# A hybrid attention layer on one core: weight splits behind the first norm, zeroing behind the norms, one early load for the expanding matrix

## The chip, the cores and the metric

The kernel runs on one core of a Trainium2 chip. TensorE (PE) multiplies, VectorE (DVE), ScalarE (ACT) and GpSimd (POOL) compute on vectors, SyncE (SP) issues the DMAs. Each engine takes its instructions in order and waits on semaphores for the others. The metric is the time of one execution on the device in microseconds; lower is better.

## What is computed

One layer: an RMS norm of x, one wide projection, three attention mixers (A, B, C) with gates, and an output projection. S = 512, D = 1024, heads of 64, everything in float32.

```python
hn = rms_norm(x, ln_g[l])
proj = jnp.einsum('bsd,dc->bsc', hn, w_in[l])
...
qa = rms_norm(qa.reshape(b, s, H_A, HEAD_DIM), g[0])
ka = rms_norm(ka.reshape(b, s, H_A, HEAD_DIM), g[1])
o_a = moba_attention(qa, ka, va.reshape(b, s, H_A, HEAD_DIM), rel_bias[OFF_A:OFF_A + H_A])
...
branches = jnp.stack([o_a.reshape(b, s, W_BR) * jax.nn.silu(ga),
                      o_b.reshape(b, s, W_BR) * jax.nn.silu(gb),
                      o_c.reshape(b, s, W_BR) * jax.nn.silu(gc)], axis=2)
br = jnp.einsum('bsiw,iwd->bsid', branches, w_branch[l])
gates = jax.nn.sigmoid(gate_logits.reshape(b, s, N_BRANCH, D_MODEL))
merged = jnp.sum(gates * br, axis=2)
x = x + jnp.einsum('bsd,de->bse', merged, w_out[l])
```

## The kernel before

Every matrix product is made of three: each float32 operand is split into a high part (hi, rounded to PE's float32r) and a low part (lo, the rest), and PE adds hi*hi, hi*lo and lo*hi. The hi part is a cast, mostly on ACT (`split_hi`, L135), the lo part a subtraction on DVE or POOL (`split_lo`, L140).

The opening (`start_x`) loads x in four tiles of 128 rows. For each, ACT squares and sums it (L211), DVE adds the epsilon (rvx, L144), POOL takes the power -0.5 (rrx, L146), DVE scales by that and by the norm's weights (xn, two halves, L216; lng are the weights spread over the partitions by PE), PE transposes xn into pt and xsc (L222), and ACT and DVE split the result into xhi and xlo. The first unit's weights (`load_w`, two k steps of 128 by 512 columns in a tile w of 128x1024, four tiles, then two tiles for V) are split too. With `early` set, DVE makes hi of every second tile (L137) and POOL lo of the others.

The work then goes through units A0, W0, R0, Z0 and so on. `project` makes q and k of a unit, four tiles t of 24 matmuls each (L500 to L502), and V in four more of half the width. After each tile of q and k, ACT copies and squares it (qn, sq), DVE sums by head (ss, L516) and adds the epsilon (rv), POOL takes the power (rr), DVE scales (qn, L527), and PE transposes (tr, L557). V's result is split straight from PSUM, in four pieces, in turn on ACT and DVE. PSUM holds two such results (pj). A0's projection is run alone; W0's fills PE during A0's attention.

`start_bias`, traced behind A0's projection, builds the rows of the position bias: a one-hot table (o32, cast to oh by POOL), a mask (mk), a small matmul (pf), and an addition (fb) that goes to DRAM scratch, from which attention loads bt. It also loads and casts emat, the matrix with which `spread` later expands a value per head to 64 columns. ws and wst are buffers of `spread` whose unused parts are zeroed once, from zer.

The order on each engine is set by a scheduler when the kernel is built; `tc.issue_after(ins)` makes the instructions in its block follow ins on ins's engine, without a semaphore. Buffers with one tag are reused in turn (`oraw` has three), so a load into one waits for the last use of what was there.

Of the kernel before, what the change touches and what calls it, by code (L numbers as in the profile page):

```python
# [9 lines left out]
F32 = mybir.dt.float32  # L10
F32R = mybir.dt.float32r
AF = mybir.ActivationFunctionType
ALU = mybir.AluOpType
# [4 lines left out]
S = 512  # L18
D = 1024
NT = 4  # L20
KT = 8
BIG = 1e30
EPS = 1e-6
WBUFS = 6
LBUFS = 4
ORAWS = 3
# [77 lines left out]
def body(tc, x, ln_g, w_in, qk_g, sinks, w_branch, w_out, rel_bias, c_ident, c_onehot, c_mask, c_expand, out):  # L104
    nc = tc.nc
    V, A, G, T = nc.vector, nc.scalar, nc.gpsimd, nc.tensor
# [7 lines left out]
    with top:  # L114
# [8 lines left out]
        emat = cp.tile([128, 2, 512], F32R, name="emat")  # L123
        mhalf = cp.tile([128, 8], F32, name="mhalf")
# [8 lines left out]
        def split_hi(dst, src, eng=A):  # L133
            if eng is A:
                A.copy(dst, src)  # L135
            else:
                eng.tensor_copy(dst, src)  # L137

        def split_lo(dst, src, hi, eng=V):
            eng.tensor_tensor(dst, src, hi.bitcast(F32), ALU.subtract)  # L140

        def rsqrt(pool, src, n, inv, tag):
            v = pool.tile([128, n], F32, name="rv" + tag, tag="rv" + tag)
            V.tensor_scalar(v, src, inv, EPS, ALU.mult, ALU.add)  # L144
            r = pool.tile([128, n], F32, name="rr" + tag, tag="rr" + tag)
            G.tensor_tensor(r, v, mhalf[:, :n], ALU.pow)  # L146
            return r

        nw = [0]
# [22 lines left out]
        def win_piece(c, n):  # L172
            return (n, lambda k0, k1: win[:, k0:k1, c : c + n])
# [3 lines left out]
        qkv = top.enter_context(tc.tile_pool(name="qkv", bufs=2))  # L177
# [5 lines left out]
        def start_x():  # L183

            lrow = qkv.tile([1, D], F32, name="lrow", tag="vhi")
            nc.sync.dma_start(lrow, ln_g)
            ones = qkv.tile([1, 128], F32, name="ones", tag="sq", bufs=1)
            V.memset(ones, 1.0)
            lng = [ps.tile([128, 512], F32, name="lng", tag="po") for _ in range(2)]
            for g in range(2):  # L190
                T.matmul(lng[g], ones, lrow[:, g * 512 : g * 512 + 512], start=True, stop=True)
            xts = []
            xsc = ps.tile([128, 2, 512], F32, name="xsc", tag="sc", bufs=1)

            def load_x(t):
                xt = qkv.tile([128, D], F32, name="xt", tag=("qhi", "qlo")[t % 2])
                nc.sync.dma_start(xt, x2[t * 128 : (t + 1) * 128, :])
                xts.append(xt)

            load_x(0)  # L200
            nc.sync.dma_start(idr, c_ident)
            for t in range(NT):
                if t == 1:
                    load_x(1)
                    w = loads(units[0], True)
                    load_x(2)
                    load_x(3)
                xt = xts[t]
                sq = qkv.tile([128, D], F32, name="xsq", tag="klo")
                ss = qkv.tile([128, 1], F32, name="xss", tag="xss")  # L210
                A.activation(sq, xt, AF.Square, accum_out=ss)  # L211
                r = rsqrt(qkv, ss, 1, 1.0 / D, "x")
                xn = qkv.tile([128, D], F32, name="xn", tag="khi")
                for g in range(2):
                    gs = slice(g * 512, g * 512 + 512)
                    V.scalar_tensor_tensor(xn[:, gs], xt[:, gs], r, lng[g], ALU.mult, ALU.mult)  # L216
                    if g:
                        pt = xsc[:, t % 2].rearrange("p (k c) -> p k c", k=4)
                    else:
                        pt = ps.tile([128, 4, 128], F32, name="pt", tag="tr")  # L220
                    for k in range(4):
                        T.transpose(pt[:, k], xn[:, (g * 4 + k) * 128 : (g * 4 + k + 1) * 128], ident)  # L222
                    dh = xhi[:, g * 4 : g * 4 + 4, t * 128 : (t + 1) * 128]
                    dl = xlo[:, g * 4 : g * 4 + 4, t * 128 : (t + 1) * 128]
                    split_hi(dh, pt)
                    split_lo(dl, pt, dh)
            return w

        def start_bias():

            rb = qkv.tile([64, 32], F32, name="rb", tag="qn", bufs=3)
            V.memset(rb, 0.0)
            nc.sync.dma_start(rb[:40, :], rel_bias)
            rp = ps.tile([32, 64], F32, name="rp", tag="po")
            T.transpose(rp, rb, ident[:64, :64])
            rt = qkv.tile([64, 64], F32R, name="rt", tag="qn", bufs=3)
            V.tensor_copy(rt[0:32], rp)
            split_lo(rt[32:64], rp, rt[0:32])
            for kinds in (("A", "W"), ("C", "R", "Z")):
                c0 = OFF[kinds[0]]  # L240
                n = sum(SPAN[k][0] for k in kinds)
                o32 = qkv.tile([64, 1024], F32, name="o32", tag="oraw", bufs=ORAWS)
                oh = qkv.tile([64, 1024], F32R, name="oh", tag="oraw", bufs=ORAWS)
                mk = qkv.tile([8, 1024], F32, name="mk", tag="oraw", bufs=ORAWS)
                fb = qkv.tile([8, 1024], F32, name="fb", tag="oraw", bufs=ORAWS)
                nc.sync.dma_start(o32[:, :n], c_onehot[:, c0 : c0 + n])
                G.tensor_copy(oh[:, :n], o32[:, :n])
                nc.sync.dma_start(mk[:, :n], c_mask[:, c0 : c0 + n])
                for k in kinds:
                    for c in range(0, SPAN[k][0], 512):  # L250
                        m = min(512, SPAN[k][0] - c)
                        o = OFF[k] + c - c0
                        pf = ps.tile([8, 512], F32, name="pf", tag="po")
                        T.matmul(pf[:, :m], rt[:, HEAD0[k] : HEAD0[k] + 8], oh[:, o : o + m], start=True, stop=True)
                        V.tensor_tensor(fb[:, o : o + m], pf[:, :m], mk[:, o : o + m], ALU.add)
                nc.sync.dma_start(scr[:, c0 : c0 + n], fb[:, :n])
            for g in range(2):
                e32 = qkv.tile([128, 512], F32, name="e32", tag="qn", bufs=3)
                nc.sync.dma_start(e32, c_expand[:, g * 512 : g * 512 + 512])
                V.tensor_copy(emat[:, g], e32)  # L260

        def start_small():
            for h in range(2):
# [176 lines left out]
        with att:  # L440
            at = att.enter_context(tc.tile_pool(name="att", bufs=2))

            zer = qkv.tile([128, 128], F32, name="zer", tag="qn", bufs=3)
            V.memset(zer, 0.0)
            revr = at.tile([128, 128], F32R, name="revr", bufs=1)
            identr = at.tile([128, 128], F32R, name="identr", bufs=1)
            ws = at.tile([128, NT, 192], F32R, name="ws", bufs=1)
            for c in range(0, 192, 32):
                G.tensor_copy(ws[:, :, c : c + 32], zer.rearrange("p (t c) -> p t c", t=NT))
            wsts = [at.tile([128, S], F32R, name=f"wst{i}", bufs=1) for i in range(2)]  # L450
            for wt in wsts:
                for c in range(0, S, 128):
                    G.tensor_copy(wt[64:128, c : c + 128], zer[64:128, :])
            pthi = at.tile([128, 1664], F32R, name="pthi", bufs=1)
            ptlo = at.tile([128, 1664], F32R, name="ptlo", bufs=1)
            V.tensor_copy(pthi[:, 1408:1536], zer)
# [396 lines left out]
            units = [(k, int(h), max("WRZ".find(k), 0)) for k, h in UNITS]  # L853

            def loads(unit, early=False):
                kind, hf, gi = unit
                c = hf * 256
                if kind == "C":
                    if hf == 0:
                        return [load_w([win_piece(QC, 256), win_piece(KC, 256)], KT)]  # L860
                    return [load_w([win_piece(QC + 256, 256)], KT)]
                if kind == "A":
                    q, k, v = QA, KA, VA
                else:
                    q, k, v = QB + gi * 512, KB + gi * 512, VB + gi * 512
                qk, vv = [win_piece(q + c, 256), win_piece(k + c, 256)], [win_piece(v + c, 256)]
                if kind in "RZ":
                    return [load_w(vv, KT), load_w(qk, KT)]
                return [load_w(qk, KT, early), load_w(vv, KT)]
# [47 lines left out]
            for ui, (kind, hf, gi) in enumerate(units):  # L917
# [5 lines left out]
                if ui not in uq:  # L923
                    run(unit_project(ui, wnext))
                    if ui == 0:
                        start_bias()
                    wnext = loads(units[ui + 1]) if ui + 1 < len(units) else None
                u = uq[ui]
                oraw = oraw_tile()
# [11 lines left out]
                name = kind + str(hf)  # L941
# [130 lines left out]
        for n in range(2, len(jobs) - 1):  # L1072
# [3 lines left out]
            w, wnext = wnext, job_load(n + 1)  # L1076
# [15 lines left out]
            else:  # L1092
                br = "ABC"[i]
                for dc in range(4):
                    tg = ("pj", "sc", "tr", "po")[dc]
                    po = gsc[0][:, 1] if tg == "sc" else ps.tile([128, 512], F32, name="po", tag=tg)
                    for k in range(4):
                        a = w[0](k)[:, dc * 128 : dc * 128 + 128]
# [77 lines left out]
```

## Time and profile before

| | |
|---|---|
| median of 3 runs (lowest to highest) | 797.91 us (796.34 to 802.05) |
| the profiled execution, its own time | 801.72 us |
| its span | 799.9 us |
| busy PE, DVE, ACT, POOL in the span | 96%, 62%, 52%, 28% |
| mean granted clock of PE | 0.991 of 2.4 GHz |

Rows of the profile name engine, line, operation, what is written and read, and the duration. What stands in square brackets is how long the engine had been idle before it and who released it. Times count from the span's start.

### The profile page before, as it was taken

The numbers are of one execution on the slowest core, as the hardware profiler recorded it, in microseconds if no ns is written. First come the engines' busy times: TensorE is split into PE (matmuls) and PEld (weight loads), VectorE is DVE, ScalarE is ACT, GpSimd is POOL, SyncE is SP. The second block draws the span as 40 slices with busy tenths as digits, with TensorE's granted clock in tenths as the row PEclk, the third lists the DMA queues.
The fourth block names the chain that finished last, engine by engine and source line by source line (L and its number), as shares of the span: only waits on it lengthen the run. The fifth ranks groups of instructions, "written<-read, shape, count | busy, mean of one in ns | idle before, by whom it ended". The sixth has DMA issues, their size and how long they took to land.

```text
span 799.9 us, 12675 instructions
## 1 busy us (share of the span) xinstructions
PE 768.9 (96%) x4727; PEld 658.4 (82%) x4727; DVE 496.9 (62%) x1068; ACT 413.3 (52%) x914; POOL 223.4 (28%) x139
## 2 busy tenths in 40 slices
PE   5989999999999989999999999899999999999998
PEld 3877788788878878878887877688899999999886
DVE  5663554546547665353655785748999787987512
ACT  4542664666566356466656656465455345445300
POOL 5573623261762372326173240101000000000000
PEclk9999999999999999999999999999999999999999
DMA  9343325153322143515332121515044324436302
GB/s 272 119 144 84 105 82 157 60 187 91 106 79 60 54 132 82 157 60 185 93 105 72 54 61 43 168 35 158 27 159 134 102 83 132 132 105 201 116 1 105
DMA packets 67473, 85.99 MB, mean 107 GB/s; under 512 B 4915, under 2 KB 53171, under 8 KB 67412
## 3 DMA queue, kind: packets, MB, share of 16 engines
q1 hardware_dynamic: 67412, 85.19, 35.0%
q8 instruction: 37, 0.61, 0.3%
q14 instruction: 24, 0.20, 0.1%
HBM read 75.67 MB, written 9.50 MB: 106 GB/s over the span
## 4 chain that ended last, share of the span: by engine, by line
PE 89%; DVE 3%; ACT 2%; DMA 2%; POOL 1%; issue 1%; SPq 0%; ACTq 0%; DVEq 0%; POOLq 0%
PE pj L500 12%; PE pj L501 12%; PE pj L502 12%; PE fc L356 11%; PE acc L1130 6%; PE fsc L356 4%; PE po L610 3%; PE pj L276 3%; PE pj L277 3%; PE pj L278 3%; PE sc L660 2%; DMA w<-in_w_in 2%; PE po L1100 2%; PE tr L680 2%; PE po L1101 2%; PE po L1102 2%
## 5 line engine op out<-in xcount | busy, mean ns | idle before, releaser
L500 PE MATMUL pj<-whi,xhi 128*128 128x512 f32 (+1 forms) x576 | 203.1, 353 | 0.9 <-DVE vhi L140 0.5
L501 PE MATMUL pj<-wlo,xhi 128*128 128x512 f32 (+1 forms) x576 | 196.8, 342 | 0.0
L502 PE MATMUL pj<-whi,xlo 128*128 128x512 f32 (+1 forms) x576 | 196.3, 342 | 0.0
L140 POOL TENSOR_TENSOR wlo<-w,whi 128x1024 fp32r<-128x1024 f32 x58 | 142.4, 2471 | 131.7 <-ACT whi L135 130.5
L135 ACT CAST whi<-w 128x1024 fp32r<-128x1024 f32 x108 | 112.9, 1050 | 78.0 <-PE fsc L356 18.8
L500 PEld LDWEIGHTS pj<-whi,xhi 128*128 128x128 f32 x576 | 109.1, 190 | 16.1 <-issue 1.2
L502 PEld LDWEIGHTS pj<-whi,xlo 128*128 128x128 f32 x576 | 109.4, 190 | 12.9 <-DVE xlo L140 0.6
L501 PEld LDWEIGHTS pj<-wlo,xhi 128*128 128x128 f32 x576 | 109.5, 190 | 11.4 <-issue 0.7
L146 POOL TENSOR_TENSOR rr<-rv,mhalf 128x8 f32<-128x8 f32 (+2 forms) x40 | 61.7, 1542 | 159.6 <-DVE rv L144 156.3
L140 DVE TENSOR_TENSOR ptlo<-tr,pthi 128x128 fp32r<-128x128 f32 (+3 forms) x112 | 51.1, 459 | 58.2 <-ACT pthi L135 37.8
L140 DVE TENSOR_TENSOR wlo<-w,whi 128x1024 fp32r<-128x1024 f32 x52 | 66.1, 1282 | 22.9 <-ACT whi L135 22.8
L135 ACT CAST pthi<-tr 128x128 fp32r<-128x128 f32 (+3 forms) x112 | 44.6, 402 | 59.0 <-PE tr L680 24.3
L527 DVE TENSOR_TENSOR qn<-qn,rr 128x512 f32<-128x512 f32 (+1 forms) x36 | 38.8, 1077 | 24.1 <-POOL rr L146 22.3
L516 DVE TENSOR_REDUCE ss<-sq 128x8 f32<-128x512 f32 (+2 forms) x40 | 25.7, 643 | 30.9 <-ACT sq L514 30.2
L356 PE MATMUL fc<-xlo,whi 128*128 128x256 f32 x144 | 40.2, 279 | 0.0
L356 PE MATMUL fc<-xhi,wlo 128*128 128x256 f32 x144 | 40.2, 279 | 0.0
L356 PE MATMUL fc<-xhi,whi 128*128 128x256 f32 x144 | 40.2, 279 | 0.0
L276 PE MATMUL pj<-xhi,whi 128*128 128x512 f32 x96 | 39.7, 413 | 0.0
L584 DVE CUSTOM_DVE_ANT_0 lg<-sc,bt 128x128 f32<-128x128 f32 (+2 forms) x96 | 28.4, 337 | 17.7 <-PE sc L660 9.5
L585 ACT ACTIVATE lg<-lg,sm 128x128 f32<-128x128 f32 (+1 forms) x80 | 32.7, 410 | 12.1 <-DVE sm L584 11.9
L277 PE MATMUL pj<-xlo,whi 128*128 128x512 f32 x96 | 38.2, 398 | 0.0
L278 PE MATMUL pj<-xhi,wlo 128*128 128x512 f32 x96 | 37.9, 395 | 0.0
(262 smaller groups left out, 1702.2 us busy)
## 6 DMA issues: line engine op xcount, KB each, us to landing
w<-in_w_in SPq DMA_DIRECT2D x54, 512.0 KB, 3.9
w<-in_w_in SPq DMA_DIRECT2D x72, 256.0 KB, 3.1
w<-in_w_branch SPq DMA_DIRECT2D x12, 512.0 KB, 3.3
vscr<-vn SPq DMA_DIRECT2D x16, 256.0 KB, 2.7
w<-in_w_out SPq DMA_DIRECT2D x8, 512.0 KB, 3.3
osp<-oraw SPq DMA_DIRECT2D x6, 512.0 KB, 2.6
oback<-osp SPq DMA_DIRECT2D x6, 512.0 KB, 4.3
xt<-in_x SPq DMA_DIRECT2D x4, 512.0 KB, 6.5
```

The costliest lines, as they stand in the source:

```text
L135: A.copy(dst, src)
L140: eng.tensor_tensor(dst, src, hi.bitcast(F32), ALU.subtract)
L146: G.tensor_tensor(r, v, mhalf[:, :n], ALU.pow)
L276: T.matmul(psum, a, xhi[:, k, :], start=(k == 0), stop=False)
L277: T.matmul(psum, a, xlo[:, k, :], start=False, stop=False)
L278: T.matmul(psum, wlo(k)[:, c : c + 128], xhi[:, k, :], start=False, stop=(k == KT - 1))
L356: T.matmul(psum[:, c], w[:, k, cs], x_[:, k, :], start=(first and c == 0 and k == 0 and q == 0), stop=(c == 1 and k == 3 and q == 2), skip ...
L500: T.matmul(pj[:, :ncol], xh, whi(k), start=(k == 0), stop=False)
L501: T.matmul(pj[:, :ncol], xh, wlo(k), start=False, stop=False)
L502: pe = T.matmul(pj[:, :ncol], xl, whi(k), start=False, stop=(k == KT - 1))
L527: V.tensor_tensor(q3[:, :nq], q3[:, :nq], r[:, :nq].unsqueeze(2).broadcast_to([128, nq, 64]), ALU.mult)
L1130: T.matmul(acc[t * 2 + e], part[k // 2][:, k % 2, tsl], wo[q](k)[:, es], start=(k == 0 and q == 0 and part is mhi), stop=(k == KT - 1 and ...
```

## The change

Four edits. The DVE instructions of the first unit's weight splits follow the second xn of x's tile 0. The cast oh of the first one-hot table follows the fourth rrx on POOL. The fourteen zeroing casts of ws and wst follow the fourth rr of A0 on POOL, and zer lies in the buffer of late. The matrix for emat is loaded by one DMA into a buffer of oraw, cast by one instruction, and the cast follows the fourth rv of A0 on DVE.

```diff
         def rsqrt(pool, src, n, inv, tag):
             v = pool.tile([128, n], F32, name="rv" + tag, tag="rv" + tag)
-            V.tensor_scalar(v, src, inv, EPS, ALU.mult, ALU.add)
+            last_rv[0] = V.tensor_scalar(v, src, inv, EPS, ALU.mult, ALU.add)
             r = pool.tile([128, n], F32, name="rr" + tag, tag="rr" + tag)
-            G.tensor_tensor(r, v, mhalf[:, :n], ALU.pow)
+            pows.append(G.tensor_tensor(r, v, mhalf[:, :n], ALU.pow))
             return r
...
                     load_x(1)
-                    w = loads(units[0], True)
+
+                    with tc.issue_after(norm.ins):
+                        w = loads(units[0], True)
...
-                    V.scalar_tensor_tensor(xn[:, gs], xt[:, gs], r, lng[g], ALU.mult, ALU.mult)
+                    norm = V.scalar_tensor_tensor(xn[:, gs], xt[:, gs], r, lng[g], ALU.mult, ALU.mult)
...
         def start_bias():
 
+            e32 = qkv.tile([128, 2, 512], F32, name="e32", tag="oraw", bufs=ORAWS)
+            nc.sync.dma_start(e32.rearrange("p a b -> p (a b)"), c_expand)
+            with tc.issue_after(last_rv[0].ins):
+                V.tensor_copy(emat, e32)
...
-                G.tensor_copy(oh[:, :n], o32[:, :n])
+                with tc.issue_after(pows[NT - 1].ins):
+                    G.tensor_copy(oh[:, :n], o32[:, :n])
...
-            for g in range(2):
-                e32 = qkv.tile([128, 512], F32, name="e32", tag="qn", bufs=3)
-                nc.sync.dma_start(e32, c_expand[:, g * 512 : g * 512 + 512])
-                V.tensor_copy(emat[:, g], e32)
...
-            zer = qkv.tile([128, 128], F32, name="zer", tag="qn", bufs=3)
+            zer = at.tile([128, 1280], F32, name="zer", tag="late", bufs=1)[:, :128]
...
-            for c in range(0, 192, 32):
-                G.tensor_copy(ws[:, :, c : c + 32], zer.rearrange("p (t c) -> p t c", t=NT))
...
-            for wt in wsts:
-                for c in range(0, S, 128):
-                    G.tensor_copy(wt[64:128, c : c + 128], zer[64:128, :])
...
                     if ui == 0:
+                        with tc.issue_after(pows[-1].ins):
+                            for c in range(0, 192, 32):
+                                G.tensor_copy(ws[:, :, c : c + 32], zer.rearrange("p (t c) -> p t c", t=NT))
+                            for wt in wsts:
+                                for c in range(0, S, 128):
+                                    G.tensor_copy(wt[64:128, c : c + 128], zer[64:128, :])
                         start_bias()
```

DVE in the opening, before; the numbers behind w tell the weight tiles apart, rvx and xn belong to the tiles of x in turn:

```order
L144 TENSOR_SCALAR rvx<-xss 128x1 x2
L137 CAST whi<-w_148 128x1024
L140 TENSOR_TENSOR wlo<-w_148,whi 128x1024
L216 SCALAR_TENSOR_TENSOR xn<-xt,rrx,lng 128x512 x4
L137 CAST whi<-w_162 128x1024
L140 TENSOR_TENSOR xlo<-pt,xhi 128x4x128
L140 TENSOR_TENSOR wlo<-w_162,whi 128x1024
```

DVE in the opening, now, where the first weight tile is w_134 and the third w_148:

```order
L146 TENSOR_SCALAR rvx<-xss 128x1
L220 SCALAR_TENSOR_TENSOR xn<-xt,rrx,lng 128x512 x2
L146 TENSOR_SCALAR rvx<-xss 128x1
L137 CAST whi<-w_134 128x1024
L220 SCALAR_TENSOR_TENSOR xn<-xt,rrx,lng 128x512
L140 TENSOR_TENSOR wlo<-w_134,whi 128x1024
L220 SCALAR_TENSOR_TENSOR xn<-xt,rrx,lng 128x512
L140 TENSOR_TENSOR xlo<-pt,xhi 128x4x128
L140 TENSOR_TENSOR xlo<-xsc,xhi 128x4x128
L137 CAST whi<-w_148 128x1024
```

Both xn of tile 0 stand ahead of the first whi, and its wlo between the two xn of tile 1.

DVE at the fourth norm of A0, before, from V's second tile to the scaling of qn by the fourth rr:

```order
L140 TENSOR_TENSOR vhi<-pj,vhi 128x2x64
L140 TENSOR_TENSOR vlo<-pj,vlo 128x2x64
L260 CAST emat<-e_618 128x512
L255 TENSOR_TENSOR fb<-pf,mk 8x512
L255 TENSOR_TENSOR fb<-pf,mk 8x128
L527 TENSOR_TENSOR qn<-qn,rr_447 128x512
```

The same stretch now, from the fourth rv on (vhi and vlo on DVE are the lower halves of V's pieces):

```order
L146 TENSOR_SCALAR rv_431<-ss 128x8
L238 CAST emat<-e_576 128x1024
L140 TENSOR_TENSOR vhi<-pj,vhi 128x2x64
L140 TENSOR_TENSOR vlo<-pj,vlo 128x2x64
L245 CAST rt<-rp 32x64
L568 SCALAR_TENSOR_TENSOR qlo<-tr,gq,qhi 128x2x128
L140 TENSOR_TENSOR vhi<-pj,vhi 128x2x64
L140 TENSOR_TENSOR rt<-rp,rt 32x64
L568 SCALAR_TENSOR_TENSOR klo<-tr,gn,khi 128x2x128
L140 TENSOR_TENSOR vlo<-pj,vlo 128x2x64
L527 TENSOR_TENSOR qn<-qn,rr_433 128x512
```

The cast of emat moved from just ahead of fb and qn to just behind rv, ahead of V's first tile.

POOL at the norms of A0, before; the four rr are those of A0's tiles 0 to 3, w_624 to w_645 are W0's weights for q and k, w_652 and w_658 those for V:

```order
L146 TENSOR_TENSOR rr_309<-rv_307,mhalf 128x8
L146 TENSOR_TENSOR rr_355<-rv_353,mhalf 128x8
L146 TENSOR_TENSOR rr_401<-rv_399,mhalf 128x8
L140 TENSOR_TENSOR wlo<-w_624,whi 128x1024
L140 TENSOR_TENSOR wlo<-w_631,whi 128x1024
L140 TENSOR_TENSOR wlo<-w_638,whi 128x1024
L140 TENSOR_TENSOR wlo<-w_645,whi 128x1024
L146 TENSOR_TENSOR rr_447<-rv_445,mhalf 128x8
L140 TENSOR_TENSOR wlo<-w_652,whi 128x1024
```

POOL at the norms of A0, now:

```order
L148 TENSOR_TENSOR rr_341<-rv_339,mhalf 128x8
L140 TENSOR_TENSOR wlo<-w_621,whi 128x1024
L148 TENSOR_TENSOR rr_387<-rv_385,mhalf 128x8
L140 TENSOR_TENSOR wlo<-w_628,whi 128x1024
L140 TENSOR_TENSOR wlo<-w_635,whi 128x1024
L140 TENSOR_TENSOR wlo<-w_642,whi 128x1024
L148 TENSOR_TENSOR rr_433<-rv_431,mhalf 128x8
L928 CAST ws<-zer 128x4x32 x6
L931 CAST wst_91<-zer 64x128 x4
L931 CAST wst_92<-zer 64x128 x4
L140 TENSOR_TENSOR wlo<-w_649,whi 128x1024
```

One wlo of W0's moved ahead of the third rr, and the zeroing stands behind the fourth.

## Rows read from the trace of the kernel before

**Rows 1.** The page's first part: busy us, share of the span, instructions of each engine.

```profile
PE 768.9 (96%) x4727; PEld 658.4 (82%) x4727; DVE 496.9 (62%) x1068; ACT 413.3 (52%) x914; POOL 223.4 (28%) x139
```

**Rows 2.** Windows of the span: busy us of each engine, granted clock, DMA share, GB/s.

```profile
0.00:20.00 20.00, 10.98 (x31) 7.13 (x32) 11.21 (x22) 9.70 (x15) 10.58 (x27) 1.00 0.90 272
...
40.00:60.00 20.00, 17.05 (x128) 15.19 (x127) 12.23 (x23) 8.60 (x19) 14.54 (x7) 0.97 0.48 144
```

**Rows 3.** Timeline of the opening: start us, us, engine, line, operation, [idle before].

```profile
1.37 1.47 POOL L449 CAST ws<-zer 128x128 fp32r<-128x128 f32 x6
...
2.91 1.98 POOL L453 CAST wst<-zer 64x128 fp32r<-64x128 f32 x8
...
6.03 0.56 POOL L146 TENSOR_TENSOR rrx<-rvx,mhalf 128x1 f32<-128x1 f32 x1 [1.14 <-DVE rvx L144]
...
10.10 0.69 DVE L137 CAST whi<-w 128x1024 fp32r<-128x1024 f32 x1 [0.24 <-DMA w<-in_w_in]
...
10.83 1.23 DVE L140 TENSOR_TENSOR wlo<-w,whi 128x1024 fp32r<-128x1024 f32 x1
...
11.97 2.72 DVE L216 SCALAR_TENSOR_TENSOR xn<-xt,rrx,lng 128x512 f32<-128x512 f32 x4
...
12.72 2.37 POOL L140 TENSOR_TENSOR wlo<-w,whi 128x1024 fp32r<-128x1024 f32 x1 [1.88 <-ACT whi L135]
...
14.61 1.03 DVE L137 CAST whi<-w 128x1024 fp32r<-128x1024 f32 x1
...
15.25 0.78 PE L500 MATMUL pj<-whi,xhi 128*128 128x512 f32 x1
...
15.66 2.38 POOL L140 TENSOR_TENSOR wlo<-w,whi 128x1024 fp32r<-128x1024 f32 x1 [0.57 <-ACT whi L135]
...
16.16 2.96 DVE L140 TENSOR_TENSOR wlo<-w,whi 128x1024 fp32r<-128x1024 f32 x1
```

**Rows 4.** Timeline of ACT at V's second weight tile and tile 2 of x.

```profile
22.76 1.05 ACT L135 CAST whi<-w 128x1024 fp32r<-128x1024 f32 x1 [0.92 <-DMA w<-in_w_in]
...
24.86 0.57 ACT L135 CAST xhi<-pt 128x512 fp32r<-128x512 f32 x1
```

**Rows 5.** Timeline of A0's projection from tile 2 to the fourth norm.

```profile
35.83 0.59 ACT L512 COPY qn<-pj 128x512 f32<-128x512 f32 x1 [2.04 <-PE pj L502]
...
40.25 9.90 POOL L140 TENSOR_TENSOR wlo<-w,whi 128x1024 fp32r<-128x1024 f32 x4
...
40.32 2.88 DVE L527 TENSOR_TENSOR qn<-qn,rr 128x512 f32<-128x512 f32 x1 [1.81 <-POOL rr L146]
...
41.82 0.59 ACT L512 COPY qn<-pj 128x512 f32<-128x512 f32 x1 [0.34 <-PE pj L502]
...
45.28 0.22 DVE L144 TENSOR_SCALAR rv<-ss 128x8 f32<-128x8 f32 x1
...
50.12 1.62 POOL L146 TENSOR_TENSOR rr<-rv,mhalf 128x8 f32<-128x8 f32 x1
...
54.56 0.43 DVE L260 CAST emat<-e 128x512 fp32r<-128x512 f32 x1 [4.24 <-DMA e<-in_c_expand]
...
55.01 2.80 POOL L140 TENSOR_TENSOR wlo<-w,whi 128x1024 fp32r<-128x1024 f32 x1 [3.27 <-ACT whi L135]
...
55.70 2.65 DVE L527 TENSOR_TENSOR qn<-qn,rr 128x512 f32<-128x512 f32 x1
...
58.41 0.88 PE L557 MATMUL tr<-idr,qn 128*128 128x128 f32 x4 [2.44 <-DVE qn L527]
```

**Rows 6.** Window behind the wait for the fourth norm.

```profile
58.00:62.00 4.00, 3.56 (x10) 2.63 (x11) 2.90 (x9) 2.28 (x6) 1.96 (x1) 0.59 0.13 34
```

**Rows 7.** Timeline of PE at W0's fourth norm.

```profile
95.31 0.66 PE L557 MATMUL tr<-idr,qn 128*128 128x128 f32 x4 [0.70 <-DVE qn L527]
```

**Rows 8.** A later unit's fourth norm on PE, and a window behind it.

```profile
295.50 0.63 PE L557 MATMUL tr<-idr,qn 128*128 128x128 f32 x4 [2.37 <-DVE qn L527]
...
298.00:300.00 2.00, 2.00 (x10) 1.19 (x8) 1.03 (x5) 1.97 (x7) 0.00 (x0) 0.50 0.00 0
```

More of the change, by code (lines that the diff above doesn't have):

```diff
@@ L140, in split_lo @@
             eng.tensor_tensor(dst, src, hi.bitcast(F32), ALU.subtract)
+        pows, last_rv = [], [None]
         def rsqrt(pool, src, n, inv, tag):
             v = pool.tile([128, n], F32, name="rv" + tag, tag="rv" + tag)
-            V.tensor_scalar(v, src, inv, EPS, ALU.mult, ALU.add)
+            last_rv[0] = V.tensor_scalar(v, src, inv, EPS, ALU.mult, ALU.add)
             r = pool.tile([128, n], F32, name="rr" + tag, tag="rr" + tag)
-            G.tensor_tensor(r, v, mhalf[:, :n], ALU.pow)
+            pows.append(G.tensor_tensor(r, v, mhalf[:, :n], ALU.pow))
             return r
```

## The prediction

> **What bounds the kernel now.** I read the page's busy times first, then the windows, then the timeline of the first 60 us engine by engine, then the order of both kernels. PE is busy for 96% of the span [rows 1], so a change gains only where PE stands still or runs at the lower of its two clocks, or where it begins earlier. The order of the two kernels differs only up to W0's projection (and by one pair of rows in the next unit), some 100 us; so I look for PE's losses there. In the first 20 us PE works 10.98 us and in 40 to 60 us 17.05 [rows 2]. That is 9 us lost at the start and 2.95 us in the middle; the rest of the span has smaller waits.
>
> The start [rows 3]: xn of the first tile needs rrx, ready at 6.59, and lng, ready by then. DVE starts xn only at 11.97, since whi and wlo of the first weight tile stand ahead of it, and these wait until 10.10 for their DMA. So PE's transposes come late too, and its first projection matmul starts at 15.25.
>
> The middle [rows 5]: DVE reaches the cast of emat and waits 4.24 us for the DMA of its source, up to 54.56. Behind it stands the scaling of the fourth tile's qn, whose rr POOL had ready at 51.74. When DVE gets there at 55.70, POOL has begun another wlo, and qn takes 2.65 us. PE waits 2.44 us for it and goes on at 58.41. From 58 to 62 us the granted clock is 0.59 [rows 6], with matmuls at 1.2 GHz after the idle stretch.
>
> **The weights' parts behind the first norm.** In the new order DVE does both xn of tile 0 before whi. They can run from 6.6, 0.68 us each (2.72 for four [rows 3]), so transposes and xhi of tile 0 are done by about 10.3 (ACT squares x tile 1 ahead of xhi). Now the first projection matmul waits for whi alone: 10.10 + 0.69, so 10.9 in place of 15.25. That is no gain of 4.3 us. The second matmul needs wlo, which stands behind one xn of tile 1: 10.79 + 0.7 + 1.23, about 12.8. The third needs xlo, behind another xn: 12.76 + 2 x 0.68, about 14.1. A matmul of 512 columns at 1.2 GHz takes 0.43 us, so until 15.25 PE has done about six (one at 10.9, two of tiles 0 and 1 from 12.8, three more up to 15.2); the transposes done by then are the same. What six matmuls are worth later is their full-clock time: tiles 2 and 3 of the projection leave 41.82 - 35.83 = 6.0 us apart for 24 matmuls and four transposes [rows 5], so 0.25 each, 1.5 us. Bounds: 0, if the opening merely runs at the lower clock for longer, and 4.3. I take **1.5 us**. It can't grow much, since the third weight tile's wlo is held by POOL in either kernel (16.16 + 2.96 = 19.12 before, by the same durations 18.6 after).
>
> ACT pays for it. In its new order both casts of V's weights stand ahead of xhi of tile 2. The second of them started at 22.76 when its DMA landed [rows 4], and the 512 KB of the expanding matrix are now ahead of it in the queue; at the 272 GB/s of the first window [rows 2] that is 1.9 us, so 24.6. From the start of that cast to xhi of tile 2 went 24.86 - 22.76 = 2.1 us; so xhi comes at 26.7 in place of 24.86. PE's work on tiles 0 and 1 lasts as long by estimate: 42 matmuls are left at 15.25, six at 0.43 and 36 at 0.25, to 26.9. The delay is hidden, but only just, and I count nothing.
>
> **Zeroing behind the norms.** Fourteen casts (1.47 + 1.98 us [rows 3]) leave POOL's first 5 us, where nothing waited: rrx began at 6.03 on DVE's word, after 1.14 us of idleness. No gain. They now stand behind the fourth rr. Behind them are two wlo for W0's values and oh; the stretch from 51.74 to the next wlo at 55 was idle before, 3.3 us, which covers them. The first reader of ws and wst is spread at the end of A0. Cost 0; without that cover 3.45 us of POOL, which W0's value weights would hide, as they are used last in W0's projection. DVE's fourth qn can meet a cast of 0.3 us, no more. oh's cast, held behind the fourth rrx, keeps its place before V's wlo: 0. zer now shares the buffer of late, which A0's softmax first writes in W0's projection, long after the casts: 0.
>
> **The expanding matrix.** One DMA of 512 KB in the opening replaces two in the middle, and one cast replaces two. It takes a buffer of oraw, so mk's DMA on SP now waits for oh's cast on POOL; behind it in SP's queue stand W0's third and fourth weight tiles, which wait for POOL's wlo of V's weights anyway: 0. DVE no longer waits for it, and the fourth rr has three wlo ahead of it since the third, not four, as one wlo moves ahead of the third rr. So the 2.95 us of waiting [rows 2] and the 4 x (1 - 0.59) = 1.64 us of lower clock [rows 6] go: **4.6 us**.
>
> But the cast stands right behind the fourth rv, where POOL runs wlo after wlo. What is late next? Call T the end of the third rr (40.25 before [rows 5]). qn of tile 2 starts at T and takes 2.88, since the first wlo holds it. ss, qlo, klo and then rv follow; before, that rv ran at 45.28, T + 5.0, just as the second wlo ended, and 0.4 earlier after, as I estimate. Now see what such instructions do against a running wlo. The cast of 128x1024 at 14.61 took 1.03 us, not 0.69, and ended 0.55 after the wlo of 12.72 + 2.37; wlo on DVE at 16.16 took 2.96 and ended 1.08 after POOL's; qn at 40.32 ended 0.55 after its first wlo [rows 3, 5]. Each did its work only when POOL's instruction was over. So rv runs at the end of the second wlo (two times 9.90 / 4, and the pause for qn: T + 5.2), the third starts, and emat's cast ends only after it: T + 7.6 + 0.6 = T + 8.2. The evacuation of V's first tile is queued behind it on DVE and alternates with ACT, four pieces of 0.3: T + 9.2. PE needs that buffer for V's third tile. Its work until then is two V tiles (half as many columns, 2.8 us each as an estimate from 6.0 with its transposes taken off), eight transposes (0.63 for four [rows 8]) and 0.6 for small matmuls, 1.9 together, from T - 0.4 on: out of work at T + 7.1. (T comes 6.3 us after tile 2's matmuls: copy 0.59, square 0.6 by estimate, then whi 1.05, wlo 2.4 and rr 1.62 in a chain, since one wlo is now ahead of this rr; tile 3 takes 6.0.) A new wait of **2.1 us** in place of one of 2.95. After a like wait of 2.37 us later in the kernel the granted clock was 0.50 [rows 8], so I charge the same 1.6 us of lower clock again (0 to 1.6). Net of this part: 4.6 - 2.1 - 1.6 = **0.9 us**. Bounds: 4.6 if the cast slips in at the boundary between two wlo, and -1.0 if it and V's evacuation are held by two.
>
> The Trainium skill bears on this place: SBUF — State Buffer, section "Who interferes with whom", says that GpSimd and VectorE share one pair of ports, that whichever instruction issues first holds it to its end, and that a cast is among those that can contend. The trace agrees in the three rows just read. By that rule the cast that the change merges into one of twice the length meets a running wlo and the sum is the forecast; by the length of the row at 14.61 alone, 0.34 us over, it would be the first rival.
>
> **W0's end.** PE waited 0.70 us at 95.31 for the fourth qn [rows 7], whose rr stood behind four wlo. Now the third and the fourth rr stand there, but PE transposes both only before the first turn of A0, and by the row durations they end about a microsecond earlier than PE comes. Gain **0.7 us** (0 to 0.7; -1 if both are late).
>
> **Sum.** 1.5 + 0.9 + 0.7 = 3.1 us. The profiled execution took 801.72 us, 799.9 of span and 1.8 around it; it becomes 798.6. It lies 3.8 above the median of 797.91; taken off that, the forecast is **794.8 us**.
>
> **Rivals.**
> - The cast is not held: the fourth rv comes a little later or the cast gets in directly behind it. For it: rv and the boundary between the two wlo are only half a microsecond apart. Then the middle gives 4.6: 1.5 + 4.6 + 0.7 = 6.8, 791.1 us. With a lead of 3 us in place of 1.5 this passes 789.9.
> - No lead at the start: the opening stays at the lower clock for as much longer as it began earlier. For it: the first matmul at 15.25 takes 0.78 us, and the third weight tile comes at the same time. 796.3 us.
> - The change does not do what it says: the new early DMA delays V's weights so far that ACT, in order, withholds xhi of tile 2 and PE stands. This is the one that ends slower. PE can absorb a landing of V's second weight tile up to about 25.6; at 27.1 a wait of 1.5 us and 1.6 us of lower clock eat the 3.1; at 29 it is 5.0, so 799.8 us. Against it: its DMA needs 3 us more than the queue's rate suggests.
>
> **How the numbers follow.** Forecast 0.45, cast not held 0.25, no lead 0.15, starved by V's weights 0.10, the rest 0.05. About 1% (8 us) is what a measurement of this kernel can tell from no change. Faster than 789.9 needs the first rival with a longer lead, or more: 0.17. Slower than 805.9 needs two delays at once: 0.05. Within: 0.78. The range goes from the first rival with 1.5 us more of lead, 789.5, to the starved case, 799.5.
>
> **What would show it.** PE's first projection matmul near 11, and the copy of tile 2's result near 34.3, not 35.83. No 4 us wait of DVE for e. The cast of emat near 2 to 3 us long with POOL's wlo beside it, PE waiting some 2 us for the evacuation of V, and the granted clock low behind it: if the cast takes 0.7, the first rival is right. V's second whi on ACT starting near 24.6. If xhi of tile 2 starts after 29 or PE's transposes of the fourth tile start later than 58.41, I am wrong.

## The result, and the profile after

| | before | after |
|---|---|---|
| median, 15 runs of each (lowest to highest) | 798.95 us (796.34 to 804.14) | 794.63 us (793.29 to 796.92) |
| ratio, 95% interval | | 0.9939 (0.9923 to 0.9955) |
| profiled execution, span | 801.72, 799.9 us | 795.95, 794.1 us |

The change takes 4.9 us off (0.0061 of 798.95; 3.6 to 6.2 by the interval). The page says where PE stands now; its windows answer to [rows 1, 2]:

```profile
PE 770.3 (97%) x4727; PEld 657.7 (83%) x4727; DVE 494.8 (62%) x1067; ACT 412.0 (52%) x914; POOL 223.8 (28%) x139
...
0.00:20.00 20.00, 15.52 (x43) 9.90 (x44) 13.35 (x26) 10.28 (x16) 7.63 (x13) 1.00 0.93 291
...
40.00:60.00 20.00, 19.43 (x140) 17.17 (x139) 11.86 (x25) 7.67 (x19) 19.42 (x22) 1.00 0.47 130
...
80.00:100.00 20.00, 18.05 (x146) 15.92 (x144) 12.83 (x32) 10.25 (x32) 6.94 (x4) 1.00 0.42 119
```

PE works 4.5 us more in the first 20 us and 2.4 us more from 40 to 60; from 80 to 100 nothing is gained (18.05 us, 18.21 before).

**The opening** in the timeline, DVE's rows first, then PE's (before: [rows 3]):

```profile
6.55 1.41 DVE L220 SCALAR_TENSOR_TENSOR xn<-xt,rrx,lng 128x512 f32<-128x512 f32 x2 [0.75 <-POOL rrx L148]
...
9.33 0.69 DVE L137 CAST whi<-w 128x1024 fp32r<-128x1024 f32 x1 [0.22 <-DMA w<-in_w_in]
10.10 0.75 DVE L220 SCALAR_TENSOR_TENSOR xn<-xt,rrx,lng 128x512 f32<-128x512 f32 x1
10.76 1.22 DVE L140 TENSOR_TENSOR wlo<-w,whi 128x1024 fp32r<-128x1024 f32 x1
...
7.35 1.12 PE L226 MATMUL pt<-idr,xn 128*128 128x128 f32 x4 [1.33 <-DVE xn L220]
...
10.17 0.77 PE L500 MATMUL pj<-whi,xhi 128*128 128x512 f32 x1 [0.85 <-DVE whi L137]
...
12.03 0.79 PE L501 MATMUL pj<-wlo,xhi 128*128 128x512 f32 x1
```

xn runs 5.4 us earlier, and the first projection matmul comes at 10.17 in place of 15.25. ACT's rows show how much of it is left further on (before: [rows 4, 5]):

```profile
24.34 1.05 ACT L135 CAST whi<-w 128x1024 fp32r<-128x1024 f32 x1
...
25.82 0.58 ACT L135 CAST xhi<-pt 128x512 fp32r<-128x512 f32 x1
...
34.02 0.58 ACT L512 COPY qn<-pj 128x512 f32<-128x512 f32 x1 [1.75 <-PE pj L502]
...
39.59 0.59 ACT L512 COPY qn<-pj 128x512 f32<-128x512 f32 x1 [0.35 <-PE pj L502]
```

The copies of tiles 2 and 3 come 1.8 and 2.2 us earlier. V's second whi no longer waits for its DMA, and PE doesn't wait for xhi.

**The middle**, DVE and then POOL from the third rr on, then PE at V's third tile and at the fourth tile's transposes (before: [rows 5]):

```profile
40.32 2.88 DVE L527 TENSOR_TENSOR qn<-qn,rr 128x512 f32<-128x512 f32 x1 [1.59 <-POOL rr L148]
...
44.51 0.97 DVE L146 TENSOR_SCALAR rv<-ss 128x8 f32<-128x8 f32 x1
45.40 0.68 DVE L238 CAST emat<-e 128x1024 fp32r<-128x1024 f32 x1
46.00 0.28 DVE L140 TENSOR_TENSOR vhi<-pj,vhi 128x128 fp32r<-128x128 f32 x1
...
40.24 5.21 POOL L140 TENSOR_TENSOR wlo<-w,whi 128x1024 fp32r<-128x1024 f32 x2
...
45.42 2.90 POOL L140 TENSOR_TENSOR wlo<-w,whi 128x1024 fp32r<-128x1024 f32 x1
...
47.04 0.36 PE L500 MATMUL pj<-whi,xhi 128*128 128x256 f32 x1 [0.57 <-DVE rt L245]
...
53.28 0.60 PE L557 MATMUL tr<-idr,qn 128*128 128x128 f32 x4
...
58.00:62.00 4.00, 4.00 (x19) 3.21 (x18) 0.26 (x2) 0.00 (x0) 1.56 (x2) 1.00 0.75 120
```

The last row is a window. rv was held for 0.97 us, to the end of POOL's second wlo at 45.45. The cast stood directly behind it and took 0.68 us: it got in ahead of the third wlo, which took 2.90 us where the first took 2.40. PE waits 0.57 us before V's third tile, and the fourth tile's transposes come at 53.28 in place of 58.41, without a wait. The granted clock from 58 to 62 us was 1.00, where before it was 0.59.

**W0's end** on PE (before: [rows 7]):

```profile
87.67 0.60 PE L557 MATMUL tr<-idr,qn 128*128 128x128 f32 x4
89.14 0.83 PE L557 MATMUL tr<-idr,qn 128*128 128x128 f32 x4 [0.86 <-DVE qlo L568]
90.66 0.55 PE L680 MATMUL tr<-idr,lg 128*128 128x128 f32 x3 [0.69 <-DVE qlo L568]
```

Two tiles are now transposed there; the waits are 0.86 and 0.69 us where they were 0.70 and 0.87. The last row, the first transposes of A0's lg behind W0's projection, stood at 96.83 before; I call it the mark, since it lies behind all that the change moves, but for one pair of rows on DVE and on ACT near 300 us. There the changed kernel is 6.2 us ahead, and 5.8 at the end of the span.

### The profile page after: what moved, and what is told of

Same layout as the page of the kernel before. It is cut to its first block, busy times and chain, and to the rows that moved or that the text cites. A ratio compares the mean times of both kernels' runs of the same rounds, so it can differ in the third digit from the quotient of the medians.

```text
span 794.1 us, 12665 instructions
## 1 busy us (share of the span) xinstructions
PE 770.3 (97%) x4727; PEld 657.7 (83%) x4727; DVE 494.8 (62%) x1067; ACT 412.0 (52%) x914; POOL 223.8 (28%) x139
## 4 chain that ended last, share of the span: by engine, by line
PE 89%; DVE 4%; ACT 2%; POOL 1%; issue 1%; DMA 1%; SPq 0%; POOLq 0%; DVEq 0%; ACTq 0%
PE pj L500 13%; PE pj L501 12%; PE pj L502 12%; PE fc L361 11%; PE acc L1136 6%; PE fsc L361 4%; PE po L610 3%; PE pj L281 3%; PE pj L282 3%; PE pj L283 3%; PE sc L660 2%; PE tr L680 2%; PE po L1106 2%; PE po L1107 2%; PE po L1108 2%; PE tr L557 2%
## 5 line engine op out<-in xcount | busy, mean ns | idle before, releaser
L527 DVE TENSOR_TENSOR qn<-qn,rr 128x512 f32<-128x512 f32 (+1 forms) x36 | 34.6, 961 | 21.5 <-POOL rr L148 21.5
```

Source lines behind the costliest of these rows:

```text
L527: V.tensor_tensor(q3[:, :nq], q3[:, :nq], r[:, :nq].unsqueeze(2).broadcast_to([128, nq, 64]), ALU.mult)
```

## Experiments

Ratios are to the kernel before; the changed kernel's is that of the result above, the others are from five rounds each. Kernels of one batch shared their runs of before, whose medians were 799.73, 799.85 and 799.31 us. The mark is read from each kernel's own timeline.

| kernel | ratio (95%) | median | mark |
|---|---|---|---|
| changed kernel | 0.9939 (0.9923 to 0.9955) | 794.63 | 90.66 |
| weights' edit alone | 1.0027 (1.0008 to 1.0046) | 802.45 | 95.72 |
| matrix's edit alone | 0.9949 (0.9929 to 0.9969) | 795.90 | 91.31 |
| zeroing's edit alone | 0.9953 (0.9934 to 0.9972) | 796.12 | 91.97 |
| changed, cast ahead of rv | 0.9960 (0.9945 to 0.9975) | 796.72 | 94.01 |
| changed, without the weights' edit | 0.9930 (0.9902 to 0.9957) | 793.99 | 90.14 |
| changed, without the zeroing's edit | 0.9999 (0.9980 to 1.0017) | 799.36 | 94.06 |
| the same, DVE's opening put right | 0.9951 (0.9934 to 0.9968) | 795.65 | 91.22 |
| changed, cast behind vlo | 0.9924 (0.9898 to 0.9951) | 794.00 | 90.47 |
| changed, POOL's splits behind rr | 0.9843 (0.9818 to 0.9868) | 788.16 | 88.27 |
| the last two together | 0.9847 (0.9824 to 0.9870) | 786.64 | 88.39 |

**Each edit alone, on the kernel before.** First the weights' edit:

```diff
-                    w = loads(units[0], True)
+                    with tc.issue_after(norm.ins):
+                        w = loads(units[0], True)
```

> The kernel before with one edit alone: the DVE splits of the first unit's weights behind the second xn. Theory (the lead is made here): PE's first projection matmul near 10.5 in place of 15.25, ACT's copy of tile 3 about 2 us earlier than 41.82, and about 2 us less in all, near 797 where the kernel before takes 799. Rival (the lead is swallowed by the wait for emat's source, whose end is set by its DMA): the copies come 2 us earlier, but PE's transposes of the fourth tile still come near 58.4, and the time is that of the kernel before.

Both theories missed: it is slower. DVE and PE in its opening:

```profile
8.40 0.15 DVE L144 TENSOR_SCALAR rvx<-xss 128x1 f32<-128x1 f32 x1 [2.52 <-ACT xsq L213]
8.53 1.41 DVE L218 SCALAR_TENSOR_TENSOR xn<-xt,rrx,lng 128x512 f32<-128x512 f32 x2
...
15.85 0.80 PE L503 MATMUL pj<-wlo,xhi 128*128 128x512 f32 x1 [1.98 <-DVE wlo L140]
```

The scheduler still put rvx of tile 1 ahead of xn of tile 0, so xn waited for the second x tile. It also put whi of the third weight tile ahead of wlo of the first; that whi started at 12.14, met POOL's wlo and took 2.52 us, and PE waited 1.98 us for wlo. ACT's copies of tiles 2 and 3 come at 38.65 and 44.16, 2.8 and 2.3 us later than before. At the mark it is 1.1 us ahead all the same, since PE still has work while DVE waits for e and its wait of 2.44 us is gone; by the ratio the whole is 2.2 us behind (0.6 to 3.7). So some 3 us go behind the mark. In the profile the granted clock from 90 to 100 us is 0.83, where it was 1.00 before; the rest goes around 300 and 445 us.

The matrix's edit alone is the diff's lines in `rsqrt` and those on e32 in `start_bias`, without oh's.

> The kernel before with one edit alone: the expanding matrix by one early DMA through a buffer of oraw and one cast behind the fourth rv. Theory (the cast gets in at the boundary between two wlo of POOL): the cast takes 0.7 us, PE's wait of 2.44 us and the lower clock behind it are gone, 3.3 to 4.1 us less in all, near 795.5 of 799. Rival (the forecast's step: the cast is held by a wlo): cast of 2 to 3 us, PE waits some 2 us for V's evacuation, 0.9 us less. In both the opening is as before, with the first projection matmul near 15.

The theory holds: 0.0051 x 799.7 = 4.1 us (2.5 to 5.7). DVE at the cast:

```profile
44.65 0.36 DVE L146 TENSOR_SCALAR rv<-ss 128x8 f32<-128x8 f32 x1
44.93 0.68 DVE L236 CAST emat<-e 128x1024 fp32r<-128x1024 f32 x1
```

Here too it came in behind rv, unheld, with a different opening ahead of it. PE's transposes of the fourth tile start at 54.52, 3.9 us earlier, and once the lower clock is gone the distance is 5.6.

The zeroing's edit alone:

> The kernel before with one edit alone: the fourteen zeroing casts behind the fourth rr, zer in the buffer of late. Theory (in the order that the scheduler then builds, both xn of tile 0 stand ahead of whi on DVE as well, so this edit makes the same lead as the weights' edit): first projection matmul near 10.5, about 2 us less, near 797 of 799. Rival (the forecast: the zeroing was worth nothing, since it lay in POOL's idle first 5 us): no change, or up to 1 us more because the casts now stand on POOL ahead of the wlo of W0.

It gains 3.8 us (2.2 to 5.3). The lead is made: first matmul at 10.28, xn at 6.53, with nothing said in the code on the order of xn and whi. It does more than the theory said. DVE waits for e as before, but 2.6 us earlier, and PE waits 1.24 us in its place:

```profile
51.94 0.47 DVE L262 CAST emat<-e 128x512 fp32r<-128x512 f32 x1 [2.94 <-DMA e<-in_c_expand]
...
55.98 0.47 PE L497 MATMUL pj<-whi,xhi 128*128 128x512 f32 x1 [1.24 <-DVE vlo L140]
```

Behind that wait the granted clock stays full: 1.00 from 58 to 62 us. Why e landed earlier can be read from SP, before and in this kernel:

```profile
48.52 0.35 SPq L259 DMA_DIRECT2D e<-in_c_expand  x1
...
47.23 0.35 SPq L261 DMA_DIRECT2D e<-in_c_expand  x1
```

In both, what SP waits for is PE's matmul rp, which reads rb, another tile in qn's three buffers (rp ends at 48.49 and 47.20). That is 1.3 us earlier, by PE's lead, and the load takes 4.7 us to its landing in place of 6.0; why it is shorter was not tried. So part of what the matrix's edit removes is gone in this kernel as well, and the gains of 4.1 and 3.8 don't add: at the mark the two edits are 5.5 and 4.9 us ahead by themselves, the changed kernel 6.2. oh's edit was never run by itself; it is in the changed kernel and in all its variants below.

**Where the cast meets POOL.** One place earlier, with rv made to follow it:

```diff
+                            with tc.issue_after(sum_.ins):
+                                done.append(V.tensor_copy(emat, e32))
+                            with tc.issue_after(done[0].ins):
+                                r = rsqrt(qkv, ss[:, :nh], nh, 1.0 / 64, str(nh))
```

> The changed kernel with emat's cast one place earlier: behind the fourth tile's sum ss, ahead of qlo, klo and the fourth rv, so that it starts near 43.8 us, inside POOL's second wlo and not at its end. Theory (an instruction of this kind that meets a running wlo waits for its end; the changed kernel's cast only slipped in behind rv): the cast takes 2.2 to 2.4 us, to 46.1; rv then meets the third wlo and ends near 48.3; V's evacuation behind it comes 2.3 us later, PE waits 2.5 to 3 us in place of 0.57 before V's third tile and runs at the lower clock behind that: 3 to 4.5 us more than the changed kernel, 797.5 to 799 where that takes 794.6. Rival (this cast is not held by a wlo at all): it takes 0.7 us, rv runs at 45.4 as in the changed kernel, and the time is that of the changed kernel.

DVE, then PE:

```profile
43.30 2.27 DVE L519 CAST emat<-e 128x1024 fp32r<-128x1024 f32 x1
...
46.28 1.53 DVE L146 TENSOR_SCALAR rv<-ss 128x8 f32<-128x8 f32 x1
47.72 0.28 DVE L140 TENSOR_TENSOR vhi<-pj,vhi 128x128 fp32r<-128x128 f32 x1
...
46.11 0.80 PE L561 MATMUL tr<-idr,qn 128*128 128x128 f32 x4 [0.76 <-DVE qlo L572]
...
48.77 0.55 PE L496 MATMUL pj<-whi,xhi 128*128 128x256 f32 x1 [1.42 <-DVE rt L241]
```

The cast is held 1.6 us, rv behind it too, PE waits 0.76 and 1.42 us, and V's third tile runs at 1.2 GHz to 52 us (granted clock 0.50 from 50 to 52). At 86 us it is 3.3 us behind the changed kernel. This is the forecast's mechanism, at nearly the forecast's price (2.1 of waiting and 1.6 of clock), in a place where the change doesn't put the cast. The median lies 2.1 us above the changed kernel's, less than the 3 to 4.5 that were expected, and the intervals overlap. In its profile the lower clock behind 289 and behind 502, which the changed kernel's shows (below), costs less: the distance falls by 1.3 us at each, to 0.7 at the end.

Two places later, behind vhi and vlo of V's first tile, nothing else moved on any engine:

```diff
-            with tc.issue_after(last_rv[0].ins):
+            with tc.issue_after(vlos[1].ins):
                 V.tensor_copy(emat, e32)
```

> The changed kernel with one DVE instruction moved: emat's cast behind vhi and vlo of V's first tile, two places later; the other engines' order is that of the changed kernel. It then starts near 46.5, inside POOL's third wlo. Theory: it is held to that wlo's end and takes 1.7 to 2 us, but V's first tile has been evacuated ahead of it, so PE's wait of 0.57 us for V's third tile is gone; what is delayed is V's second tile, which PE needs 2.8 us later: the time is that of the changed kernel or 0.5 us less, so a held cast costs nothing in this place. Rival (what is queued behind it still comes too late): a wait of 1 us or more at V's fourth tile or at rp, and 1 to 2 us more.

DVE and PE:

```profile
46.33 2.12 DVE L238 CAST emat<-e 128x1024 fp32r<-128x1024 f32 x1
...
46.56 0.36 PE L500 MATMUL pj<-whi,xhi 128*128 128x256 f32 x1
```

The cast starts inside the third wlo and is held 1.4 us; PE's wait is gone, and no other comes: 0.9924 against 0.9939, not slower, and no more than that can be told. The profile had put that wait down to rt on DVE. Here rt ran at 48.37, later than V's third tile started, so it was V's evacuation that PE had waited for. A held cast thus costs nothing here that can be told: what counts is what stands behind it on DVE.

**Which edit makes the lead.** The changed kernel without the weights' edit:

> The changed kernel without its first edit: the block that puts the weights' DVE splits behind the second xn is taken out, the rest stays. Theory (that edit does nothing once the zeroing is moved: the scheduler then puts xn ahead by itself, and the order of all five engines is row for row that of the changed kernel): ratio to the kernel before as that of the changed kernel, 0.994 within 0.002, with the first projection matmul near 10.3. Rival (the edit makes the lead, as the forecast had it): the lead of 2 us is gone, 0.9965.

The order of all five engines is row for row the changed kernel's, and the time agrees. The same order run twice shows what the clock does later on. The windows of the changed kernel, then of this one:

```profile
290.00:300.00 10.00, 9.22 (x53) 8.13 (x55) 4.82 (x16) 5.23 (x16) 0.00 (x0) 0.66 0.34 83
...
500.00:510.00 10.00, 8.08 (x40) 6.77 (x41) 7.05 (x15) 4.21 (x14) 2.31 (x1) 0.83 0.31 102
```

```profile
290.00:300.00 10.00, 9.52 (x62) 8.29 (x63) 5.68 (x18) 5.16 (x16) 0.00 (x0) 0.76 0.30 61
...
500.00:510.00 10.00, 8.58 (x52) 7.30 (x53) 7.39 (x18) 4.90 (x17) 1.25 (x1) 1.00 0.39 119
```

Their spans are 794.1 and 791.8. Of the 2.3 us, 0.5 stand at the mark already; some 0.6 arise between 288 and 298 and 1.3 between 502 and 506, behind waits of the same length (2.28 and 2.31 us, then 1.92 in both), by the clock.

The changed kernel without the zeroing's edit, and then that kernel with DVE's order put right by hand:

> The changed kernel without the edit on the zeroing: the fourteen casts stay at POOL's start, zer stays in a buffer of qn. Theory (moving the zeroing is what lets the scheduler put xn of tile 0 ahead of rvx of tile 1; without it xn waits for the second x tile, as it did with the weights' edit alone): xn of tile 0 near 8.5 in place of 6.55, first projection matmul near 12.2 and a wait of some 2 us for wlo behind it, copy of tile 3 near 41; between the kernel before and the changed one, 796 to 798 where that takes 794.6. Rival (the zeroing is worth nothing, as forecast): as the changed kernel, 794.6.

```diff
-                split_hi(hi, w, V if early and nw[0] % 2 else A)
+                with tc.issue_after(xlos[1].ins) if nw[0] == 3 else nullcontext():
+                    split_hi(hi, w, V if early and nw[0] % 2 else A)
...
-                r = rsqrt(qkv, ss, 1, 1.0 / D, "x")
+                with tc.issue_after(norm.ins) if t == 1 else nullcontext():
+                    r = rsqrt(qkv, ss, 1, 1.0 / D, "x")
```

> The changed kernel with the zeroing casts left at POOL's start, as before, but DVE's opening order put right by hand: rvx of tile 1 follows the second xn of tile 0, and whi of the third weight tile follows the second xlo of tile 0. Theory (the zeroing's 3.5 us on POOL cost nothing on the chip; what moving them gained is the order on DVE that the scheduler then chose): xn of tile 0 near 6.55 though the casts stand ahead of rrx, first projection matmul near 10.3, no wait of 2 us for wlo behind it, and within 1.5 us of the changed kernel's 794.6. Rival (POOL's time matters): near 799, as with the weights' and the matrix's edits alone.

Without the zeroing's edit the whole gain is gone: 0.9999, with xn at 9.26 and a wait of PE of 1.99 us for wlo at 16.21. 3.4 us of the distance to the changed kernel stand at the mark, and one more arises between 299 and 343 us, where its order differs too. With the zeroing still at POOL's start but DVE's order mended, 3.9 us (2.6 to 5.3) come back. POOL, DVE and PE of the mended one:

```profile
1.37 1.48 POOL L456 CAST ws<-zer 128x128 fp32r<-128x128 f32 x6
2.92 1.98 POOL L460 CAST wst<-zer 64x128 fp32r<-64x128 f32 x8
6.04 0.57 POOL L148 TENSOR_TENSOR rrx<-rvx,mhalf 128x1 f32<-128x1 f32 x1 [1.14 <-DVE rvx L146]
...
6.64 1.41 DVE L222 SCALAR_TENSOR_TENSOR xn<-xt,rrx,lng 128x512 f32<-128x512 f32 x2 [0.75 <-POOL rrx L148]
...
12.29 0.79 PE L507 MATMUL pj<-whi,xhi 128*128 128x512 f32 x1 [2.87 <-ACT xhi L135]
```

POOL is done with the zeroing 1.14 us ahead of rrx, and xn runs as in the changed kernel. The first matmul was expected at 10.3 and came at 12.29, since ACT's order put whi ahead of xhi here. ACT's copy of tile 2, here and then with the matrix's edit alone:

```profile
35.19 0.59 ACT L519 COPY qn<-pj 128x512 f32<-128x512 f32 x1 [1.80 <-PE pj L509]
...
35.19 0.59 ACT L514 COPY qn<-pj 128x512 f32<-128x512 f32 x1 [1.80 <-PE pj L504]
```

They agree, and so do those of tile 3 (41.19 and 41.17), the two marks (91.22 and 91.31) and the ratios (0.9951 and 0.9949). So what came back is the matrix's gain, which DVE's order under the weights' edit had eaten, and not the lead: this run shows that the zeroing's time on POOL delays nothing, and that the loss lay in that order; it does not show what the lead is worth.

**A better version.** The same kind of wait as at W0's end stands at 289, for W1, in both kernels: 2.37 us before [rows 8], 2.28 after, for qn, whose rr stands on POOL behind wlo of a later unit:

```profile
289.28 0.63 PE L557 MATMUL tr<-idr,qn 128*128 128x128 f32 x4 [2.28 <-DVE qn L527]
```

In A0 and A1 these wlo were made to follow the last rr:

```diff
-                        wnext = loads(units[ui + 2]) if ui + 2 < len(units) else None
+                        with tc.issue_after(pows[-1].ins) if name in WB else nullcontext():
+                            wnext = loads(units[ui + 2]) if ui + 2 < len(units) else None
```

> The changed kernel, and in A0 and A1 POOL's splits of the unit after next follow the fourth rr of the unit whose projection fills PE (W0, W1), so that this rr no longer stands behind four wlo. Theory (PE's wait of 2.28 us for qn at 289, the two of 0.9 and 0.7 at 89 to 91, and the lower clock behind the first come from there): these waits go, 3 to 5 us less than the changed kernel, near 790.5. Rival (the splits that are now later are needed first): PE waits for wlo of R0 and R1 at the start of their projections instead, and the time is that of the changed kernel or more.

It takes 788.16 us, 5.8 below the changed order's 793.99 in the same batch, more than expected. POOL now takes W1's last rr as soon as rv is there, ahead of the four wlo; the window stands below:

```profile
276.82 1.64 POOL L149 TENSOR_TENSOR rr<-rv,mhalf 128x8 f32<-128x8 f32 x1 [0.50 <-DVE rv L147]
278.42 9.86 POOL L141 TENSOR_TENSOR wlo<-w,whi 128x1024 fp32r<-128x1024 f32 x4
...
290.00:300.00 10.00, 10.00 (x86) 9.21 (x85) 4.28 (x14) 5.22 (x14) 1.17 (x1) 1.00 0.42 123
```

PE's wait at 289 is gone; the granted clock from 290 to 300 is 1.00 where it was 0.66. PE is 3.7 us ahead of the changed kernel at 285 (2.4 at the mark, where one of W0's two waits is gone) and 8.9 at 298, in single executions, and the rival's new waits for wlo don't come. With the cast behind vlo as well:

> The kernel in which POOL's splits follow the fourth rr (788.2 us) with emat's cast moved behind vhi and vlo of V's first tile as well. Theory: PE's wait of 0.57 us for V's third tile goes here too, 787.6. Rival: the held cast delays something that the first move made tight, 788.2 or more.

786.64 us, but the ratio is the same, so what the second move adds is not resolved.

## Why the prediction came out as it did

The forecast of 794.8 us lies beside the measured 794.63, but not by the right sum. It expected 3.1 us and the change gave 4.9; and it started from a median of three runs, 797.91, where the same kernel took 798.95 in fifteen and 799.3 to 799.9 in the later batches. The profiled 801.72 us lay 2 to 3 us above those, not 3.8. The two errors, between 1 and 2 us each, cancel: that the number came out so near is luck.

- **The matrix: mechanism right, place wrong.** The step that failed is "the third starts, and emat's cast ends only after it". A cast that meets a running wlo is held, 2.27 and 2.12 us in two experiments. But rv's end is the wlo's end, and the cast directly behind rv got in ahead of the next wlo: 0.68 us in all six kernels that have it there, with four different openings. That is the first rival's condition, "directly behind it", which had 0.25. By itself the part is worth 4.1 us (5.5 at the mark), not 0.9; the rival's price was 4.6.
- **The opening: the lead near, its cause and its worth wrong.** The copy of tile 2 was forecast at 34.3 and came at 34.02; the lead there is 1.8 us, 1.5 were forecast. But the edit that was priced for it does nothing beside the zeroing's edit, and alone costs 2.2 us (0.6 to 3.7). Nor does the 1.5 us reach the end: against the matrix's edit alone PE leads by 1.6 us at 40 us and, behind its wait of 0.57 us for V's third tile, by 0.9 at 50. At the mark 91.31 - 90.66 = 0.65 us are left, 1.17 in the other kernel of the same order; in the medians it isn't resolved.
- **The zeroing: right on POOL, wrong as a price.** Its 3.45 us of casts are free at POOL's start, as forecast. The edit was still not worth 0 beside the weights' edit, because the order that the scheduler built for DVE hung on it: without it the gain is gone. Beside the matrix's edit alone its worth is not resolved (0.9930 against 0.9949).
- **W0's end: the 0.7 us did not come.** With two tiles' transposes there, the waits sum to 0.86 + 0.69 = 1.55 us; they were 1.57. That both rr "end about a microsecond earlier than PE comes" was nearly so (86.95 us, against 87.67), but not enough: PE next waited for qlo.
- **Starved by V's weights: no.** The second whi came at 24.34 (24.6 was forecast) with no wait for its DMA.
- **The sum again.** The matrix's 5.5 and the 0.65 left to the opening make the 6.2 us at the mark; in the span 5.8 of them remain. The medians' 4.9 has both within or at the end of its interval; the clock's dips behind 289 and 502 make single executions of one order differ by about 2. What stays open is why the two kernels with the weights' edit and the early zeroing lose 3 us more behind the mark, in the medians, while the one with the cast ahead of rv, level with one of them at the mark, doesn't. In the profiles the weights' edit alone loses 0.9 us between 97 and 110 us, 1.0 around 298 and 0.7 around 447, and the kernel without the zeroing's edit 1.8 between 296 and 345, where its order differs; the reason isn't shown.

## What to carry to other kernels

Where a scheduler sets the order, price the order that it builds with an edit and without it, not the edit's text: here one edit changed nothing, and one on another engine decided the opening. A DVE instruction that a running wlo of POOL would hold belongs directly behind one that was just held, or where nothing urgent is queued behind it; a place earlier cost 3.3 us at once. And before fine work on an opening, look for the same wait in later units: the edit for those of W0 and W1 was worth 5.8 us, about as much as the whole change.

## What the runs showed of the hardware

DVE's instructions are not all alike against a running wlo of POOL. The sum ss, from SBUF, took 0.64 us beside one, and the pieces of V out of PSUM 0.28, while rv with 8 columns took up to 2.01 us where 0.17 is its usual time. The Trainium skill, SBUF — State Buffer, section "Who interferes with whom", lists casts and tensor_scalar among those that can contend and says that tensor_reduce never does; these rows agree, and so do the casts held to 2.27 and 2.12 us. What happens at the boundary between two POOL instructions I had not expected: in all six kernels with the cast behind rv, DVE's second instruction took 0.68 us and came first though POOL's next wlo was queued.

The same wait is followed by losses of different size. Behind 2.28 and 2.31 us of waiting at 289, in two kernels of one order, the granted clock of the window from 290 was 0.66 and 0.76; behind 502 it was 0.83 and 1.00.
